# Second layer of a two-layer decoder trunk: where the value projection stands among the attention projections

## The chip, the cores and the metric

The kernel runs on one core of a Trainium2 chip. Its time is the device time of one execution in microseconds (us), and lower is better. Five engines work side by side, each through its own list of instructions in the order written: TensorE (PE; its weight loads are listed as PEld), VectorE (DVE), ScalarE (ACT), GpSimd (POOL) and SyncE (SP), which here issues transfers. What one engine needs from another it waits for.

## The reference, cut to what matters

Two layers with 512 tokens and width 1024, everything in float32. The change touches the second layer's mixer alone:

```python
proj = x @ od_w_in[o]
xr, gr, qd, kd, vd = split_cols(proj, [LRU_WIDTH, LRU_WIDTH, HALF, HALF, HALF])
yc = rg_lru_branch(xr, gr, ...)              # conv of width 4, two gates, linear scan, GeLU gate
yd = stick_breaking_attention(qd, kd, vd)    # 8 heads of 64
mix = jnp.concatenate([yc, yd], axis=-1) @ od_w_out[o]
...
# stick_breaking_attention, a block of 128 queries against the keys up to its end
z = einsum('bhqd,bhkd->bhqk', q, k) * scale
log_one_minus = where(mask, log_sigmoid(-z), 0.0)
suffix = cumsum(log_one_minus, reverse=True) - log_one_minus
w = where(mask, exp(log_sigmoid(z) + suffix), 0.0)
out = einsum('bhqk,bhkd->bqhd', w, v)
```

A head's sums z and their logarithms need only its q and k. The values v enter in the last product.

## The kernel before, in words

Every large product is made of three fp32r matmuls per 128-row block (`mm3`, L252 to L254): high by high, high by low, low by high. A weight chunk of 128 x 1024 arrives in `ws` (two buffers) by an SP transfer; ACT casts it to its high part (L241) and DVE subtracts to get the low part (L242). One projection of a chunk over all tokens (`proj`) is 24 matmuls of 128 x 512 into a PSUM bank `pj`, of which there are two. The value projection (`values`, L289 its copies) takes four chunks and is 96 such matmuls into banks `pv`, which share these two banks.

The second layer (`layer1`) runs as follows.

1. `griffin`, the recurrent branch. Four column groups j. Each has a convolution on DVE into a tile `xc` (L858, L860), two gate matmuls (`pa` L862, `px` L864), sigmoids and a tanh on ACT (L866 to L869), a logarithm part that goes back and forth between ACT (L882, L883, L889, L890) and DVE (L879, L884 to L894), a scan on DVE (L895), and, after one GeLU over all four groups on ACT (L900), a product, a cast and a subtraction (L907, L247, L248). PE makes the four `gr` projections meanwhile. `xc`, `dn` and `w` take their buffers from tag `l`, `r` from tag `z`.
2. The value projection.
3. Four pairs of heads (`sb_pair`). For each, `qk_pair` makes the q and the k projection and lays them out as `qk` tiles, with the low part of k in two `kz` tiles (L723 to L732: six instructions on ACT, four on DVE). The sums z of a pair are five tiles of 128 x 512. Each tile goes through z on PE (L933 to L935), three functions on ACT (L937 to L939), an addition, a reversed scan and a subtraction on DVE (L940, L943, L944), a "turn" (four PE transposes L951 into `pt`, an Exp on ACT L957 into `pT`), and then all five serve the products with v (L964).

The program is written in this order, and a scheduler then lists the instructions of each engine by its own estimate of when they can start; nothing reorders the list on the chip. The scheduler puts a pair's turns between the matmuls of the next pair's projections. A tile waits for its buffer until the last reader of the tile that had it is through.

Of the kernel before, what the change touches and what calls it, by code (L numbers as in the profile page):

```python
# [44 lines left out]
S_GR, S_QD, S_KD, S_VD, S_WO1 = S_XR + 4, S_XR + 8, S_XR + 12, S_XR + 16, S_XR + 20  # L45
# [11 lines left out]
class Trunk:  # L57
# [853 lines left out]
        return ys  # L911


    def sb_pair(self, hp, v):
        nc = self.nc
        A = nc.scalar.activation
        q, k = self.qk_pair(S_QD + hp, S_KD + hp, self.kz)
        yh, yl = self.act("yh"), self.act("yl")
        po = self.bank("ho", "po")


        tiles = (((0, 3, 0),), ((1, 3, 0),), ((0, 2, 0), (0, 0, 384)), ((1, 2, 0), (1, 0, 384)), ((0, 1, 0), (1, 1, 256)))
        pT = self.t2k("pT", [P, 20 * P], tag="pT")
        at = ((15, -6), (1, 5))
        rev = lambda a: a[:, ::-1]
        for ti, parts in enumerate(tiles):
            tag = "zl"[ti % 2]
            l = self.t2k("l", tag=tag)
            ps = self.bank(("s", "s", "sc")[ti % 3], "z")
            for e, i, o in parts:  # L930
                n = (i + 1) * P
                c = slice(i * P, n)
                nc.tensor.matmul(ps[:, o:o + n], q[e][:, c], k[e][:, 0:n], start=True, stop=False)  # L933
                nc.tensor.matmul(ps[:, o:o + n], q[e][:, c], self.kz[e][:, 0:n], start=False, stop=False)
                nc.tensor.matmul(ps[:, o + i * P:o + n], self.identb, self.sbmask, start=False, stop=True)  # L935

            A(l, ps, AF.Abs)  # L937
            A(l, l, AF.Exp, scale=-1.0)
            A(l, l, AF.Ln, bias=self.one)  # L939
            nc.vector.scalar_tensor_tensor(l, ps, 0.0, l, ALU.max, ALU.add)  # L940
            for e, i, o in parts:
                r = rev(l[:, o:o + (i + 1) * P])
                nc.vector.tensor_tensor_scan(r, self.ones1[:, 0:(i + 1) * P], r, 0.0, ALU.mult, ALU.add)  # L943
            nc.vector.tensor_tensor(l, ps, l, ALU.subtract)  # L944
            pt = self.bank(("pt", "po")[ti % 2], "pt")
            for e, i, o in parts:
                b, step = at[e]
                for j in range(i + 1):

                    m = j if step > 0 else i - j  # L950
                    nc.tensor.transpose(pt[:, o + m * P:o + (m + 1) * P], l[:, o + j * P:o + (j + 1) * P], self.ident)  # L951
            for e, i, o in parts:
                b, step = at[e]
                lo = b + i + (0 if step > 0 else i * step)
                dst = bass.AP(tensor=pT.tensor, offset=pT.offset + lo * P,
                              ap=[pT.ap[0], [abs(step) * P, i + 1], [1, P]])
                A(dst, pt[:, o:o + (i + 1) * P].rearrange("p (j t) -> p j t", t=P), AF.Exp)  # L957
        cp = self.newest()

        for j in range(NTB):  # L960
            for e in range(2):
                h = 2 * hp + e
                x = (at[e][0] + at[e][1] * j + j) * P
                nc.tensor.matmul(po[64 * e:64 * e + 64, j * P:T], v[j][:, h * 64:h * 64 + 64], pT[:, x:x + T - j * P],  # L964
                                 start=j == 0, stop=j == NTB - 1)
                if j == 0 and e == 0:
                    self.behind(self.newest(), cp)
        self.put(po, yh, yl)
        return yh, yl

    def layer1(self, xr):
        self.qk4 = False

        self.kz = [self.t2k("kz", dt=F32R, tag="kz") for _ in range(2)]
        for e in range(2):
            self.nc.gpsimd.memset(self.kz[e][64 - 64 * e:P - 64 * e].bitcast(F32), 0.0)
        self.ones1 = self.t2k("ones", tag="one")
        self.nc.gpsimd.memset(self.ones1, 1.0)
        yc = self.griffin(xr)
        self.hp = 600  # L980
        v = self.values(S_VD)
        self.hp = 600
        yd = []
        for hp in range(4):
            yd.append(self.sb_pair(hp, v))
            if hp == 3:
                self.out_rows(yc, S_WO1)
        self.hp = 1
        return yd


@with_exitstack
def hybrid_trunk_kernel(ctx: ExitStack, tc: tile.TileContext, out, **ins):
    t = Trunk(tc, ctx, ins, out)
    t.setup()
    with t.phase("l0", v=8, p=2, pT=1, E=5, bb=1, kq=1, G=1, acc=1, ks=1, es=1) as t.ph, \
            tc.tile_pool(name="odd", bufs=1) as t.odd:
        y = t.layer0()
    with t.phase("f0", s=2, d=1, fm=12, wah=4, wal=4) as t.ph:
        wa = t.out_rows(y, S_WO0 + 4, 0, S_FFN0)  # L1000
        wa = t.ffn(S_FFN0, wa, 1, S_XR)
        xr = t.proj_halves(wa)
    with t.phase("l1", v=4, qk=7, kz=2, z=5, l=4, pT=2, one=1) as t.ph:
        y = t.layer1(xr)
    with t.phase("f1", s=2, d=1, fm=12, wah=4, wal=4) as t.ph:
        wa = t.out_rows(y, S_WO1 + 4, 2, S_FFN1)
        t.ffn(S_FFN1, wa, 3)
# [105 lines left out]
```

## Time and profile before

| | |
|---|---|
| median of 3 runs | 1221.72 us (1219.8 to 1224.15) |
| the profiled execution | 1221.14 us, of which 1219.3 us lie between its first and last instruction |
| PE busy | 1196.5 us (98%) |
| DVE, ACT, POOL busy | 757.4 (62%), 518.6 (43%), 55.8 us (5%) |
| mean granted TensorE clock | 0.995 |
| second layer's mixer | griffin's gates from 676, value projection from 701, first pair's sums from 736 to 763, fourth pair's last products at 825 us |

How to read it: a line names the source line, the engine, the operation and what it writes and reads. Times in a timeline count from the span's start. Matmuls overlap in the record (one of 128 x 512 lasts 0.39 us, and the next starts 0.23 us after it), so the rate of work is read from starts. In the rows of stretches, the first number is the stretch's length, and behind it stands what each engine was busy in it, then the granted TensorE clock (1.00 is full), the share of the DMA engines and GB/s.

### The profile page before, as it was taken

Reading aid. Unit: us, or ns where it says so; the run is one execution under the profiler, and the core shown is the slowest. Engines: PE = TensorE matmul, PEld = TensorE weight load, DVE = VectorE, ACT = ScalarE, POOL = GpSimd, SP = SyncE. Lnnn points to the kernel's source line nnn. Section 1 sums busy time; section 2 is a strip of 40 time slices with the busy share of each in tenths; the row PEclk is TensorE's granted clock in tenths of the full one; section 3 lists DMA queues with packets and bytes.
Section 4 is the critical chain, followed back from the end, with each engine's and each line's share of the span. In section 5 each row is a group of like instructions: output and inputs, shape, how many; then the busy total and the mean of one; then the engine's idle time right before and its main releaser. Section 6 shows DMA issues by size and latency. Waiting matters only on the chain.

```text
span 1219.3 us, 15337 instructions
## 1 busy us (share of the span) xinstructions
PE 1196.5 (98%) x6063; PEld 970.6 (80%) x6063; DVE 757.4 (62%) x1141; ACT 518.6 (43%) x790; POOL 55.8 (5%) x80
## 2 busy tenths in 40 slices
PE   9999999999999999999999998999999999999997
PEld 6787777778888888878889786677988888888886
DVE  7638798769355634554368876887753644456346
ACT  7447568443233423332233667872332433333220
POOL 1000000001001000200000000000000100010001
PEclk9999999999999999999999999999999999999999
DMA  6421211233637432643324222112644643464321
GB/s 244 150 75 53 87 44 50 65 122 99 230 92 121 134 104 87 106 132 108 91 82 156 68 74 83 35 35 87 199 164 93 115 139 91 100 104 138 104 69 69
DMA packets 38727, 127.96 MB, mean 105 GB/s; under 512 B 4592, under 2 KB 6128, under 8 KB 38656
## 3 DMA queue, kind: packets, MB, share of 16 engines
q1 hardware_dynamic: 32496, 108.44, 28.0%
q0 software_dynamic: 4864, 16.81, 8.3%
q10 hardware_dynamic: 1296, 1.73, 0.4%
q8 instruction: 48, 0.79, 0.3%
q14 instruction: 23, 0.19, 0.1%
HBM read 124.84 MB, written 2.10 MB: 104 GB/s over the span
## 4 chain that ended last, share of the span: by engine, by line
PE 88%; DVE 4%; ACT 3%; DMA 2%; issue 1%; SPq 0%; DVEq 0%; ACTq 0%
PE pf L253 13%; PE pf L252 13%; PE pf L254 13%; PE pj L252 4%; PE pj L253 4%; PE pj L254 4%; PE po L254 4%; PE po L253 4%; PE po L252 4%; PE fa L252 2%; PE fa L254 2%; PE fa L253 2%; PE pv L253 2%; PE pv L252 2%; PE pv L254 2%; DMA wwal<-in_wst 1%
## 5 line engine op out<-in xcount | busy, mean ns | idle before, releaser
L241 ACT CAST wh<-ws 128x1024 fp32r<-128x1024 f32 x143 | 150.2, 1051 | 304.9 <-PE pf L253 121.8
L242 DVE TENSOR_TENSOR wl<-ws,wh 128x1024 fp32r<-128x1024 f32 x143 | 174.8, 1223 | 153.5 <-ACT wh L241 149.9
L252 PE MATMUL pf<-xh,wh 128*128 128x512 f32 x640 | 249.0, 389 | 0.0
L253 PE MATMUL pf<-xl,wh 128*128 128x512 f32 x640 | 249.0, 389 | 0.0
L254 PE MATMUL pf<-xh,wl 128*128 128x512 f32 x640 | 249.0, 389 | 0.0
L254 PEld LDWEIGHTS pf<-xh,wl 128*128 128x128 f32 x640 | 120.2, 188 | 25.0
L253 PEld LDWEIGHTS pf<-xl,wh 128*128 128x128 f32 x640 | 120.2, 188 | 24.9
L252 PEld LDWEIGHTS pf<-xh,wh 128*128 128x128 f32 x640 | 120.2, 188 | 24.7
L527 DVE TENSOR_TENSOR s<-s,pf 128x512 f32<-128x512 f32 x44 | 30.3, 688 | 148.0 <-PE pf L254 148.0
L252 PE MATMUL pj<-xh,wh 128*128 128x512 f32 x256 | 104.2, 407 | 2.1 <-DVE qk L726 2.1
L254 PE MATMUL pj<-xh,wl 128*128 128x512 f32 x256 | 104.0, 406 | 0.0
L253 PE MATMUL pj<-xl,wh 128*128 128x512 f32 x256 | 103.5, 404 | 0.2 <-DVE xl L248 0.2
L247 ACT CAST wh<-wwah 128x1024 fp32r<-128x1024 f32 x32 | 33.7, 1052 | 74.8 <-PE pf L253 63.3
L252 PEld LDWEIGHTS pj<-xh,wh 128*128 128x128 f32 x256 | 48.5, 190 | 13.6 <-DVE qk L726 2.6
L254 PEld LDWEIGHTS pj<-xh,wl 128*128 128x128 f32 x256 | 48.4, 189 | 10.3 <-issue 1.6
L253 PEld LDWEIGHTS pj<-xl,wh 128*128 128x128 f32 x256 | 48.5, 189 | 9.8 <-issue 1.0
L252 PE MATMUL po<-wh,yh 128*128 128x512 f32 x128 | 51.4, 401 | 0.0
L252 PE MATMUL fa<-wh,fm 128*128 128x512 f32 x128 | 50.0, 390 | 1.2 <-ACT wh L247 1.2
L253 PE MATMUL po<-wl,yh 128*128 128x512 f32 x128 | 51.0, 399 | 0.0
L254 PE MATMUL po<-wh,yl 128*128 128x512 f32 x128 | 50.9, 398 | 0.0
L248 DVE TENSOR_TENSOR wl<-wwah,wh 128x1024 fp32r<-128x1024 f32 x32 | 38.7, 1221 | 18.5 <-ACT wh L247 17.9
L254 PE MATMUL fa<-wh,fm 128*128 128x512 f32 x128 | 49.8, 389 | 0.0
(275 smaller groups left out, 2237.4 us busy)
## 6 DMA issues: line engine op xcount, KB each, us to landing
ws<-in_wst SPq DMA_DIRECT2D x165, 512.0 KB, 3.5
wwah<-in_wst POOLq DMA_DIRECT2D x24, 512.0 KB, 5.6
gb<-in_lnp SPq DMA_DIRECT2D x8, 512.0 KB, 5.1
wwah<-in_wst SPq DMA_DIRECT2D x8, 512.0 KB, 5.9
wwal<-in_wst SPq DMA_DIRECT2D x8, 512.0 KB, 6.8
wwal<-in_wst POOLq DMA_DIRECT2D x8, 512.0 KB, 6.1
ws<-in_wst SPq DMA_DIRECT2D x11, 256.0 KB, 5.2
xt<-in_xT SPq DMA_DIRECT2D x8, 256.0 KB, 5.2
```

The source lines that it names most:

```text
L241: nc.scalar.copy(hi, st)
L242: nc.vector.tensor_tensor(lo, st, hi.bitcast(F32), ALU.subtract)
L247: self.nc.scalar.copy(hi, dst)
L248: self.nc.vector.tensor_tensor(lo, dst, hi.bitcast(F32), ALU.subtract)
L252: mm(ps, ah, bh, start=first, stop=False, **kw)
L253: mm(ps, ah, bl, start=False, stop=False, **kw)
L254: mm(ps, al, bh, start=False, stop=last, **kw)
L527: nc.vector.tensor_tensor(h, h, pb, ALU.mult)
```

## The change

The first pair's projections and sums now stand ahead of the value projection, and so do the second pair's projections. `sb_pair` is called for pair 0 with a function `between`: the five z tiles are carried through their logarithms and kept; then `between` makes the second pair's `qk` tiles and the value projection; then the five turns follow. There are four `kz` tiles, two for even and two for odd pairs, and eight `qk` buffers instead of seven. Tag `z` has four buffers instead of five and tag `l` three instead of four, and the tile of ones that the scan read is gone: the scan reads a 128 x 1 column of ones, repeated.

```diff
-    def sb_pair(self, hp, v):
+    def sb_front(self, hp):
+        return self.qk_pair(S_QD + hp, S_KD + hp, self.kz[hp % 2])
+
+    def sb_pair(self, hp, v, front=None, between=None):
...
-        q, k = self.qk_pair(S_QD + hp, S_KD + hp, self.kz)
+        q, k = front or self.sb_front(hp)
+        kz = self.kz[hp % 2]
...
+        def turn(ti, parts, l):
+            pt = self.bank(("pt", "po")[ti % 2], "pt")
...
-                nc.vector.tensor_tensor_scan(r, self.ones1[:, 0:(i + 1) * P], r, 0.0, ALU.mult, ALU.add)
+                nc.vector.tensor_tensor_scan(r, self.one.to_broadcast([P, (i + 1) * P]), r, 0.0, ALU.mult, ALU.add)
...
+            if between:
+                ls.append((ti, parts, l))
+            else:
+                turn(ti, parts, l)
+        if between:
+            v = between()
+            for x in ls:
+                turn(*x)
...
-        self.kz = [self.t2k("kz", dt=F32R, tag="kz") for _ in range(2)]
...
+        self.kz = [[self.t2k("kz", dt=F32R, tag="kz") for _ in range(2)] for _ in range(2)]
...
         yc = self.griffin(xr)
         self.hp = 600
-        v = self.values(S_VD)
...
+        def between():
+
+            front.append(self.sb_front(1))
+            v.extend(self.values(S_VD))
+            return v
+
         for hp in range(4):
-            yd.append(self.sb_pair(hp, v))
+            yd.append(self.sb_pair(hp, v, front[0] if hp == 1 else None, between if hp == 0 else None))
...
-    with t.phase("l1", v=4, qk=7, kz=2, z=5, l=4, pT=2, one=1) as t.ph:
+    with t.phase("l1", v=4, qk=8, kz=4, z=4, l=3, pT=2) as t.ph:
```

How the lists of the engines stand. The first place is PE, from griffin's last projection (`pj_944`) to the first sums of pair 0 (`z_990`), before; `pv_969` and `pv_972` are the first and the last bank of the value projection, `pj_980` and `pj_984` the first pair's projections of q and k, `pj_1011` the second pair's q.

```order
L254 MATMUL pj_944_5773<-xh_83,wl_943_5770 128x512
L252 MATMUL pv_969_5849<-wh_958_5827,xh_83 128x512
...
L254 MATMUL pv_972_5927<-wh_967_5845,xl_84 128x512
L252 MATMUL pj_980_5963<-xh_83,wh_978_5959 128x512
...
L254 MATMUL pj_984_5998<-xh_83,wl_983_5995 128x512
L252 MATMUL pj_1011_6153<-xh_83,wh_1009_6149 128x512
...
L933 MATMUL z_990_6034<-qk_975_5955,qk_973_5953 128x512
```

In this list the value projection and two chunks' projections, 144 matmuls, lie between griffin's last projection and the second pair's q, and nine more ahead of the first sums. The same place of the changed kernel: `pj_945` is griffin's last projection, `pj_961` and `pj_965` the first pair's q and k, `z_971` its first sums, `pj_987` the second pair's q.

```order
L254 MATMUL pj_945_5775<-xh_83,wl_944_5772 128x512
L252 MATMUL pj_961_5833<-xh_83,wh_959_5829 128x512
...
L254 MATMUL pj_965_5868<-xh_83,wl_964_5865 128x512
L954 MATMUL z_971_5904<-qk_956_5825,qk_954_5823 128x512
L954 MATMUL z_975_5926<-qk_956_5825,qk_954_5823 128x384
L252 MATMUL pj_987_5980<-xh_83,wh_985_5976 128x512
L253 MATMUL pj_987_5980<-xl_84,wh_985_5976 128x512
L254 MATMUL pj_987_5980<-xh_83,wl_986_5977 128x512
L955 MATMUL z_971_5904<-kz_888_5503,qk_954_5823 128x512
```

Now 48 matmuls lie between griffin's last projection and the first sums, and the second pair's q stands behind these.

The second place is PE around the value projection (`pv_1008` to `pv_1011`) of the changed kernel. `pt_1012` to `pt_1016` are the five turns of pair 0, `z_1022` the first sums of pair 1.

```order
L254 MATMUL pj_991_6015<-xh_83,wl_990_6012 128x512
L938 MATMUL pt_1012_6178<-ident_66,l_970_5903 128x128 x4
L938 MATMUL pt_1013_6184<-ident_66,l_972_5914 128x128 x4
L938 MATMUL pt_1014_6190<-ident_66,l_974_5925 128x128 x4
L938 MATMUL pt_1015_6197<-ident_66,l_976_5940 128x128 x4
L954 MATMUL z_1022_6226<-qk_982_5972,qk_980_5970 128x512
L954 MATMUL z_1028_6260<-qk_982_5972,qk_980_5970 128x384
L938 MATMUL pt_1016_6204<-ident_66,l_978_5955 128x128
L252 MATMUL pv_1008_6074<-wh_997_6052,xh_83 128x512
...
L254 MATMUL pv_1011_6152<-wh_1006_6070,xl_84 128x512
L938 MATMUL pt_1016_6204<-ident_66,l_978_5955 128x128 x3
L955 MATMUL z_1022_6226<-kz_890_5505,qk_980_5970 128x512
```

Four of the five turns, and the start of the fifth, stand ahead of the 96 matmuls of the value projection; the completion of pair 1's first sums stands behind them.

The third place is DVE at griffin's end. Before, its last instructions were followed by the splitting of weights:

```order
L895 SCALAR_TENSOR_TENSOR ig_899_5544<-w_928_5658,ig_899_5544 128x512
L248 TENSOR_TENSOR yl_946_5803<-ig_899_5544,yh_945_5802 128x512
L907 TENSOR_TENSOR ig_899_5544<-ig_899_5544,ig_900_5545 128x512
...
L248 TENSOR_TENSOR yl_952_5818<-ig_899_5544,yh_951_5817 128x512
L242 TENSOR_TENSOR wl_983_5995<-ws_981_5992,wh_982_5994 128x1024
```

Nothing but griffin's own work stood there. Now the list holds a third value chunk's split (`wl_1004`) and the second half of q (`qk_955`) between them, and the low parts of k (`kz_888`, `kz_889`) directly behind:

```order
L895 SCALAR_TENSOR_TENSOR ig_900_5546<-w_929_5660,ig_900_5546 128x512
L242 TENSOR_TENSOR wl_1004_6065<-ws_1002_6062,wh_1003_6064 128x1024
...
L248 TENSOR_TENSOR yl_951_5815<-ig_900_5546,yh_950_5814 128x512
L726 SCALAR_TENSOR_TENSOR qk_955_5824<-pj_961_5833,qk_955_5824 64x512
L248 TENSOR_TENSOR yl_953_5820<-ig_900_5546,yh_952_5819 128x512
L732 TENSOR_TENSOR kz_888_5503<-pj_965_5868,qk_956_5825 64x512
L732 TENSOR_TENSOR kz_889_5504<-pj_965_5868,qk_957_5826 64x512
```

From griffin's first L884 to the last `yl`, DVE splits two weight chunks before the change and four after it, and two L726 are new in that stretch.

More of the change, by code (lines that the diff above doesn't have):

```diff
@@ L925, in sb_pair @@
         rev = lambda a: a[:, ::-1]
[L926 to L944, printed above, removed]
+        def turn(ti, parts, l):
             pt = self.bank(("pt", "po")[ti % 2], "pt")
@@ L957, in sb_pair @@
                 A(dst, pt[:, o:o + (i + 1) * P].rearrange("p (j t) -> p j t", t=P), AF.Exp)
+        ls = []
+        for ti, parts in enumerate(tiles):
+            tag = "zl"[ti % 2]
+            l = self.t2k("l", tag=tag)
+            ps = self.bank(("s", "s", "sc")[ti % 3], "z")
+            for e, i, o in parts:
+                n = (i + 1) * P
+                c = slice(i * P, n)
+                nc.tensor.matmul(ps[:, o:o + n], q[e][:, c], k[e][:, 0:n], start=True, stop=False)
+                nc.tensor.matmul(ps[:, o:o + n], q[e][:, c], kz[e][:, 0:n], start=False, stop=False)
+                nc.tensor.matmul(ps[:, o + i * P:o + n], self.identb, self.sbmask, start=False, stop=True)
+            A(l, ps, AF.Abs)
+            A(l, l, AF.Exp, scale=-1.0)
+            A(l, l, AF.Ln, bias=self.one)
+            nc.vector.scalar_tensor_tensor(l, ps, 0.0, l, ALU.max, ALU.add)
+            for e, i, o in parts:
+                r = rev(l[:, o:o + (i + 1) * P])
+                nc.vector.tensor_tensor_scan(r, self.one.to_broadcast([P, (i + 1) * P]), r, 0.0, ALU.mult, ALU.add)
+            nc.vector.tensor_tensor(l, ps, l, ALU.subtract)
+            if between:
[6 more added lines that the diff above has]
+                turn(*x)
         cp = self.newest()
@@ L972, in layer1 @@
         self.qk4 = False
-        self.kz = [self.t2k("kz", dt=F32R, tag="kz") for _ in range(2)]
[L975 to L978, printed above, removed]
+        self.kz = [[self.t2k("kz", dt=F32R, tag="kz") for _ in range(2)] for _ in range(2)]
+        for kz in self.kz:
+            for e in range(2):
+                self.nc.gpsimd.memset(kz[e][64 - 64 * e:P - 64 * e].bitcast(F32), 0.0)
         yc = self.griffin(xr)
         self.hp = 600
-        v = self.values(S_VD)
-        self.hp = 600
-        yd = []
+        yd, v, front = [], [], []
+        def between():
+            front.append(self.sb_front(1))
+            v.extend(self.values(S_VD))
+            return v
         for hp in range(4):
-            yd.append(self.sb_pair(hp, v))
+            yd.append(self.sb_pair(hp, v, front[0] if hp == 1 else None, between if hp == 0 else None))
             if hp == 3:
```

## The prediction

> **What bounds the kernel now.** First the page's head and the list of waits on PE.
>
> ```profile
> span 1219.3 us, 15337 instructions
> PE 1196.5 (98%) x6063; PEld 970.6 (80%) x6063; DVE 757.4 (62%) x1141; ACT 518.6 (43%) x790; POOL 55.8 (5%) x80
> PE pt L951 <- DVE l L944: 4.6, 9, 0.8
> PE pj L252 <- DVE qk L726: 2.1, 1, 2.1
> ```
>
> PE is busy throughout; 22.8 us of the span are idle on it. The two longest waits are the second layer's: turns that wait for DVE's logarithms, and one projection that waits until its PSUM bank is read by L726. Matmuls cannot get fewer by this change, so all that it can move is PE's idle time. I therefore read the second layer stretch by stretch.
>
> ```profile
> 690.00:701.05 11.05, 11.05 (x51) 9.14 (x49) 9.53 (x15) 6.63 (x12) 0.00 (x0) 1.00 0.26 90
> 701.05:711.95 10.90, 10.90 (x49) 8.74 (x47) 10.87 (x20) 10.70 (x14) 0.00 (x0) 1.00 0.17 53
> 711.95:723.11 11.16, 11.16 (x50) 9.12 (x49) 8.67 (x12) 5.77 (x9) 0.00 (x0) 1.00 0.06 7
> 736.31:763.12 26.81, 22.66 (x114) 15.94 (x114) 19.82 (x29) 20.07 (x36) 0.00 (x0) 0.94 0.19 60
> 763.12:782.48 19.36, 18.13 (x100) 13.05 (x98) 16.11 (x23) 15.36 (x28) 0.00 (x0) 1.00 0.13 32
> 782.48:805.38 22.90, 21.27 (x115) 15.21 (x113) 18.92 (x26) 18.43 (x34) 0.00 (x0) 1.00 0.20 64
> 752.00:756.00 4.00, 0.93 (x5) 0.61 (x5) 3.64 (x6) 3.78 (x7) 0.00 (x0) 1.00 0.19 33
> 757.40:760.80 3.40, 3.40 (x13) 2.29 (x12) 1.55 (x3) 2.55 (x6) 0.00 (x0) 0.52 0.00 0
> ```
>
> Pair 0 (736.31 to 763.12) loses 26.81 - 22.66 = 4.15 us on PE, pairs 1 and 2 lose 1.23 and 1.63. Pair 0 also loses clock: after the sparse 752 to 756, 3.4 us run at 0.52, which is 3.4 x 0.48 = 1.6 us of work. So at most 5.75 us can be won there. The value projection (701.05 to 723.11) has no idle time, and it is not empty cover: in its first half DVE is busy 10.87 of 10.90 us and ACT 10.70. It hides the end of griffin.
>
> **The change: the first sums lose this cover.** What feeds them now:
>
> ```profile
> 701.05 0.39 PE L252 MATMUL pv<-wh,xh 128*128 128x512 f32 x1
> 723.11 0.39 PE L252 MATMUL pj<-xh,wh 128*128 128x512 f32 x1
> 692.66 0.68 DVE L884 TENSOR_TENSOR dn<-dn,w 128x512 f32<-128x512 f32 x1
> 716.80 1.47 DVE L248 TENSOR_TENSOR yl<-ig,yh 128x512 fp32r<-128x512 f32 x2
> 710.15 1.28 ACT L903 ACT_TABLE_LOAD   x1
> 736.35 0.68 DVE L732 TENSOR_TENSOR kz<-pj,qk 64x512 fp32r<-64x512 f32 x1
> 696.95 1.22 DVE L242 TENSOR_TENSOR wl<-ws,wh 128x1024 fp32r<-128x1024 f32 x1
> 698.08 0.42 DVE L894 TENSOR_SCALAR w<-w 128x512 f32<-128x512 f32 x1
> 729.63 0.68 DVE L726 SCALAR_TENSOR_TENSOR qk<-pj,qk 64x512 fp32r<-64x512 f32 x1
> ```
>
> *PE's arrival.* 96 matmuls take 723.11 - 701.05 = 22.06 us, 0.23 each. In place of `pv` the first pair's 48 projection matmuls start at 701.05 and are through at 701.05 + 48 x 0.23 = 712.1; with 0.5 us from the smaller tag (below), 712.6. The next instructions in PE's list are the sums z of pair 0.
>
> *When their operands are there.* ACT makes the k tiles only behind griffin's GeLU, table load and first casts, of which the table load ends at 710.15 + 1.28 = 711.4 today. DVE makes `kz` directly behind griffin's last `yl`, which ends at 716.80 + 1.47 = 718.27. From the first L884 at 692.66 to there DVE has 25.6 us, almost all busy, so what is added there is paid: two more L242 (one starts at 696.95 and the instruction behind it at 698.08, so 1.13 us each) and two L726 (0.68 long, 0.60 with the same overlap), which is 3.46 us, so 29.1.
>
> *The start moves too.* With three `l` buffers griffin's fourth `xc` must wait for the first to be read.
>
> ```profile
> 673.22 4.03 DVE L860 SCALAR_TENSOR_TENSOR xc<-xp,par,xc 128x511 f32<-128x511 f32 x6
> 682.53 0.68 DVE L871 TENSOR_TENSOR ig<-ig,xc 128x512 f32<-128x512 f32 x1
> 684.39 0.42 DVE L879 TENSOR_SCALAR dn<-r 128x512 f32<-128x512 f32 x1
> 687.41 0.67 ACT L868 ACTIVATE ig<-px,par 128x512 f32<-128x512 f32 x1
> 691.39 0.63 ACT L883 ACTIVATE w<-w 128x512 f32<-128x512 f32 x1
> ```
>
> DVE reads the first `xc` at 682.53. From there to the end of the fourth `xc` the new list has this read, two more like it, three L860 (4.03 / 6 = 0.67 each) and three short ones like L879; at 0.6, 0.67 and 0.35 apiece that is 4.9 us, so about 687.4. Its gate matmuls (about 0.9 us) and three ACT functions of 0.6 to 0.7 then end at about 690.1 instead of 687.41 + 0.67 = 688.1. The following L883 thus falls 2.0 us later than 691.39, and the first L884 with it: 694.7. PE loses little of this, since ten matmuls are listed ahead of the late gates: 0.5 us is my estimate, between 0 and the whole 2.0.
>
> So `kz` is ready at 694.7 + 29.1 + 0.7 = 724.5. Until then PE has two first parts of z and three matmuls of the second pair's q, five of 0.23, so 1.2 us. **New wait at the first sums: 724.5 - 712.6 - 1.2 = 10.7 us.** Behind the waiting z stand the second pair's 48 matmuls and the 96 of `pv`, which need nothing that is late; the list is fixed, so they wait, and with them ACT's copies of v and all later products. Bounds: with no extra DVE work and no late start, `kz` is there at 719.0 and PE at 712.1, so 719.0 - 712.1 - 1.2 = 5.7; with 2 us of bubbles where a DVE instruction needs the one just ahead of it, 12.7.
>
> *Pair 0's own chain.* It now runs under the second pair's 48 projection matmuls, as it did before, and not under the value projection: four of five turns stand ahead of `pv`. Only the last turn's exponentials and the products are covered. So PE waits there again, less than 4.15 us, since the last turn is no longer waited for, and hardly less than pair 1's 1.23. I take 3.0, nearer to pair 0's row, because the next work and the chain are the same; both ends stay in the range. During `pv` itself ACT and DVE will be nearly idle.
>
> *The clock.* The row at 752 shows what about 4 us of thin work is followed by: 3.4 us at half clock. A wait of 10.7 us should bring that at least once: 1.6 us, nothing if that stretch waits for DVE anyway, 3.3 if it comes twice.
>
> [...]
>
> *Edits that I cost at nothing.* The scan's ones: a scan reads 512 elements in 1.22 us, a product of two tiles in 0.68.
>
> ```profile
> 741.86 1.23 DVE L943 TENSOR_TENSOR_SCAN l<-ones,l 128x512 f32<-128x512 f32 x1
> L907 DVE TENSOR_TENSOR ig<-ig,ig 128x512 f32<-128x512 f32 x4 | 2.7, 680 | 0.0
> ```
>
> It is slower than its reads, so a repeated column should not change it; were it as much as 10% slower or faster, 20 full-length scans' worth of work (2560 elements per pair, 24.6 us in all) would move by 2.5 us on DVE, part of it in front of turns, which the range holds. Two more `kz` memsets for one of the ones lie on POOL, which is busy 55.8 us in all. Transfers keep their number and places in SP's list; only the chunks in them change order. Four `z` and eight `qk` buffers: a pair holds three `z` and four `qk`, and the list of the later pairs is nearly the old one, so nothing.
>
> Sum: 10.7 + 0.5 + 3.0 + 1.6 - 5.75 = **+10.05 us**. On the profiled execution's own 1221.14 us that is 1231.2; it stands 0.6 below the median of 1221.72, so I say 1231.
>
> **The rivals.**
>
> *Faster: the value projection covers the chain.* If `kz` were ready when PE arrives, nothing would be waited for at the first sums, and pair 0 would lose what pair 1 loses: 1.23 - 5.75 = -4.5, 1216.6. For it: pair 0's chain is the layer's worst stretch, and 22 us without a wait are moved. Against it: DVE would have to be through 12 us earlier, with 10.87 of 10.90 us filled. It decides where the wait at the first sums falls below 4.5 us; even the lower bound is 5.7.
>
> *No change.* The wait at its lower bound 5.7, pair 0 like pair 1 and no half clock: 5.7 + 1.23 - 5.75 = +1.2, 1222.3. For it: the scheduler's list interleaves, so DVE could find room; against it: the two splits and two L726 are listed ahead of `kz`.
>
> *Much worse: griffin starves on three `l` tiles, and the clock stays low.* `dn` and `w` of two groups need four. If each later group waits once more for its buffers, `kz` comes 2 us later still; with 2.0 on PE from the fourth `xc`, 4.15 kept and half clock twice: 12.7 + 2.0 + 4.15 + 3.3 - 5.75 = +16.4, 1237.5. For it: ACT already waits 4.08 us for DVE there with four tiles.
>
> ```profile
> 701.20 0.64 ACT L882 ACTIVATE w<-dn 128x512 f32<-128x512 f32 x1 [4.08 <-DVE dn L879]
> ```
>
> Against it: DVE is the busy engine, and reordering its work does not lengthen it. [...]
>
> *That the change doesn't do what it says* holds in part: the second pair's sums are not ahead, only their first parts, as the list shows. This is in the 3.0 above.
>
> **How the numbers follow.** Forecast 0.70; much worse 0.15; no change 0.08; faster 0.07. Both of the first are slower: 0.85. A change under 0.3% (3.7 us) cannot be told from none: 1218.1 to 1225.4. The range that should hold the time 8 times in 10 runs from 1224.5, which takes in part of the case of no change, to 1237, just under the worst case; the forecast's own range is 1227 to 1235.
>
> **What would show it.** In the changed kernel's profile: a PE wait of 8 to 12 us at the first z (L954 or L955), ended by ACT's k tile (L731) or DVE's `kz` (L732), near 713 to 724; the last `yl` of griffin at 722 to 724 instead of 718.3; a stretch of granted clock near 0.5 just behind it and none near 757; DVE and ACT nearly idle for 15 us under `pv`; pairs 1 to 3 as now. I am wrong if PE's wait at the first sums is under 5 us, if the turns ahead of `pv` cost more than 4 us, or if the scan's duration changes.

## The result and the profile after

The changed kernel takes 1230.83 us (median of 6 runs, 1230.22 to 1232.97); the kernel before, run beside it, 1221.11 us (median of 6, 1218.68 to 1224.15). The ratio is 1.0083 with a 95% interval of 1.0066 to 1.0099: slower, by 9.7 us, where +10.05 had been forecast.

The profiled execution took 1232.97 us. First its page's head and the longest waits of PE in the second layer (us in total, times, longest).

```profile
span 1231.2 us, 15345 instructions
PE 1199.1 (97%) x6063; PEld 972.7 (79%) x6063; DVE 757.9 (62%) x1141; ACT 518.0 (42%) x790; POOL 55.3 (4%) x81
PE z L954 <- ACT qk L731: 10.4, 2, 8.9
PE pt L938 <- DVE l L965: 4.2, 10, 0.8
```

The work is the same, and a wait that no row of before has heads the list. Its 10.4 us lie in two places: 8.92 us at the first sums, and the rest, 1.45 us, at pair 1's first sums (at 746.43). At the first sums a second wait follows, of 1.05 us. Here is PE at that place, and the copy on ACT that it first waits for:

```profile
722.73 1.11 PE L954 MATMUL z<-qk,qk 128*128 128x512 f32 x2 [8.92 <-ACT qk L731]
724.89 0.77 PE L252 MATMUL pj<-xh,wh 128*128 128x512 f32 x1 [1.05 <-DVE qk L726]
726.31 0.77 PE L955 MATMUL z<-kz,qk 128*128 128x512 f32 x1
722.10 0.58 ACT L731 CAST qk<-pj 64x512 fp32r<-64x512 f32 x1
```

So PE stands still for 8.92 + 1.05 = 9.97 us: first for ACT's copy of k, then for the PSUM bank that DVE's L726 has still to read. Ahead of the first matmul with `kz` (L955) there is no wait. The expectations of e2, e5, e6 and e8 call this wait 10.4 us; that is the sum over both places. To see what it is worth, the same work is cut out of both: from the start of griffin's first product into `px` (677.63 us before, 678.87 after) to the first product with v of pair 1. The stretches of before, from the start of `pv` on, and the whole:

```profile
701.05:736.31 35.26, 35.14 (x154) 28.38 (x153) 25.81 (x37) 23.61 (x31) 0.00 (x0) 1.00 0.28 91
736.31:760.81 24.50, 20.35 (x97) 14.87 (x97) 18.71 (x27) 18.97 (x35) 0.00 (x0) 0.93 0.21 65
760.81:780.13 19.32, 18.09 (x98) 12.80 (x97) 15.98 (x23) 14.87 (x28) 0.00 (x0) 1.00 0.10 28
677.63:780.13 102.50, 97.00 (x438) 72.89 (x436) 79.79 (x117) 75.02 (x120) 0.00 (x0) 0.98 0.21 67
```

And of after, cut where PE arrives at the first z (713.81), where its first matmul with `kz` starts (726.31), where `pv` starts (747.20) and where pair 0's products start (770.33):

```profile
678.87:702.29 23.42, 23.32 (x89) 16.40 (x88) 17.94 (x28) 17.46 (x27) 0.00 (x0) 1.00 0.18 53
...
713.81:726.31 12.50, 2.53 (x5) 1.36 (x6) 12.05 (x19) 9.34 (x12) 0.00 (x0) 0.69 0.18 59
726.31:747.20 20.89, 18.12 (x88) 13.50 (x87) 16.48 (x24) 15.94 (x28) 0.00 (x0) 0.94 0.10 27
747.20:770.33 23.13, 23.13 (x105) 18.80 (x105) 3.80 (x4) 6.50 (x13) 0.00 (x0) 1.00 0.13 44
770.33:791.84 21.51, 19.89 (x108) 15.02 (x107) 18.92 (x25) 17.51 (x32) 0.00 (x0) 1.00 0.32 100
678.87:791.84 112.97, 98.50 (x440) 74.28 (x438) 80.71 (x117) 74.71 (x120) 0.00 (x0) 0.95 0.20 61
```

The same work takes 112.97 - 102.50 = 10.47 us more. Of this PE is idle for 14.47 instead of 5.50 us, 8.97 more, and busy for 1.50 us more, of which the half clock is 0.85 (worked out below, with the prediction). Behind this stretch nothing more is lost: from there to the last matmul it is 431.3 us before and 431.5 after. Under the value projection (747.20 to 770.33) PE is full, and DVE with 3.80 of 23.13 us and ACT with 6.50 have next to nothing to do. The 22 us that hid griffin's end now hide little.

The profiled execution is 2 us above the median of its kernel; 1.24 us of that (678.87 - 677.63) are there by griffin's first gate, ahead of all that the change touches. Of this 1.0 us is there after 20 us, where PE in this execution waited 0.8 and 0.3 us for its first casts; across the first layer's half clock, 6.83 us in this execution (from 237.37) and 3.41 in the one of before (from 238.41), 1.1 more is added, and 0.9 goes off again by 677.

### The profile page after: what moved, and what is told of

Same layout as the page of the kernel before. It is cut to its first block, busy times and chain, and to the rows that moved or that the text cites. A ratio compares the mean times of both kernels' runs of the same rounds, so it can differ in the third digit from the quotient of the medians.

```text
span 1231.2 us, 15345 instructions
## 1 busy us (share of the span) xinstructions
PE 1199.1 (97%) x6063; PEld 972.7 (79%) x6063; DVE 757.9 (62%) x1141; ACT 518.0 (42%) x790; POOL 55.3 (4%) x81
## 4 chain that ended last, share of the span: by engine, by line
PE 87%; DVE 7%; ACT 3%; DMA 2%; issue 1%; SPq 0%; DVEq 0%; ACTq 0%
PE pf L253 13%; PE pf L252 13%; PE pf L254 13%; PE po L254 4%; PE po L253 4%; PE po L252 4%; PE pj L252 4%; PE pj L253 4%; PE pj L254 4%; PE fa L252 2%; PE fa L254 2%; PE fa L253 2%; PE pv L253 2%; PE pv L252 2%; PE pv L254 2%; DVE l L964 1%
## 5 line engine op out<-in xcount | busy, mean ns | idle before, releaser
L254 PEld LDWEIGHTS pj<-xh,wl 128*128 128x128 f32 x256 | 48.4, 189 | 10.6 <-issue 1.8
```

What stands on the lines that cost most here:

```text
L254: mm(ps, al, bh, start=False, stop=last, **kw)
```

## The experiments

The theory: the value projection covered the end of griffin on DVE and ACT; with the sums ahead of it, PE waits about 10 us at the first z. Two rivals stand against it: the buffers (three `l`, the scan over one repeated column), and the turns, which are held back behind five sums. Another question is asked by itself: how much of the loss is the half clock. Line numbers in the experiments' rows can lie a few lines off those above, since each kernel has its own text.

All medians, beside those of the kernel before on the same chip, with the profiled stretch from the start of the first `px` to the start of the last matmul (before: 533.8 us), which leaves out what differs ahead of griffin's gates:

| kernel | us | before | ratio, 95% interval | `px` to the end, against before |
|---|---|---|---|---|
| the change | 1230.83 | 1221.11 | 1.0083 (1.0066 to 1.0099) | +10.6 |
| e1, tiles alone | 1220.06 | 1220.40 | 1.0000 (0.9990 to 1.0009) | 0.0 |
| e3, values first | 1219.44 | 1220.40 | 0.9997 (0.9987 to 1.0006) | +0.2 |
| e2, four logs | 1227.81 | 1220.40 | 1.0058 (1.0043 to 1.0073) | +7.9 |
| e6, late splits | 1230.31 | 1220.65 | 1.0075 (1.0062 to 1.0089) | +10.2 |
| e8, drains first | 1224.87 | 1220.15 | 1.0044 (1.0031 to 1.0056) | +5.4 |
| e5, wait filled | 1231.04 | 1220.15 | 1.0094 (1.0079 to 1.0109) | +10.3 |
| e4, values split | 1232.49 | 1220.40 | 1.0098 (1.0083 to 1.0113) | +12.1 |
| e9, split, other banks | 1223.09 | 1220.15 | 1.0024 (1.0015 to 1.0032) | +1.8 |
| e10, and drains first | 1220.42 | 1220.15 | 0.9999 (0.9990 to 1.0008) | -0.1 |
| e11, and second front | 1219.19 | 1220.65 | 0.9987 (0.9978 to 0.9996) | -1.9 |
| e12, second front last | 1218.10 | 1220.65 | 0.9978 (0.9969 to 0.9987) | -2.1 |
| e13, late fourth sum | 1217.16 | 1220.47 | 0.9972 (0.9962 to 0.9981) | -2.9 |

### Is it the order? The tiles alone, and the values put back

```diff
 # e1: the changed kernel, in the old order
-            yd.append(self.sb_pair(hp, v, front[0] if hp == 1 else None, between if hp == 0 else None))
+        v = self.values(S_VD)
+            yd.append(self.sb_pair(hp, v))
 # e3: the changed kernel, with the values ahead of everything
-        yd, v, front = [], [], []
+        yd, v, front = [], self.values(S_VD), []
-            v.extend(self.values(S_VD))
```

> The changed kernel's tiles (two sets of key tiles, eight q and k buffers, four of the sums' z, three of the logs, and the running sum that multiplies by the one repeated column), in the old order: griffin, the value projection, then pair after pair. Theory (the value projection used to hide griffin's tail, and the order alone lost it): 1221 to 1224 us, that is 0 to 3 us over the kernel before, with no wait over 2 us at the first z and the one half-rate stretch about where it was, near 757 us. Rival (the smaller set of log buffers and the repeated column make the kernel slower, by late griffin gates and longer scans): 1228 us or more, and the running sum of 512 columns takes longer than its 1.23 us.

> The change with one thing put back: the value projection comes ahead of the first pair's projections and sums again. What stays of the change is its tiles, the five sums in a row, the second pair's projections behind them and the five turns last. Theory: the value projection covers griffin's tail as before, the wait at the first z is under 2 us, and pair 0's own waits for logs are shorter: 1219 to 1224 us. Rival (holding the turns back behind five sums, or the second pair's early projections, cost the time): 1226 us or more, with the loss between pair 0's sums and its outputs.

Both came out as the theory says: no difference from the kernel before. PE in the 34 us from 711 to 745 of e1, and of e3:

```profile
711.00:745.00 34.00, 33.58 (x154) 26.82 (x154) 23.07 (x29) 24.17 (x36) 0.00 (x0) 1.00 0.33 108
```

```profile
711.00:745.00 34.00, 33.48 (x152) 26.73 (x151) 23.08 (x29) 23.89 (x35) 0.00 (x0) 1.00 0.33 106
```

PE is busy for all but half a microsecond, where the changed kernel loses 11.31 us of the same window:

```profile
711.00:745.00 34.00, 22.69 (x101) 16.47 (x99) 29.21 (x44) 25.12 (x37) 0.00 (x0) 0.85 0.16 47
```

So the tiles cost nothing under the old cover, and neither do the turns held back. e1 also has the repeated column: its scan of 512 elements takes 1.22 us (1.23 with the tile of ones).

```profile
739.23 1.22 DVE L964 TENSOR_TENSOR_SCAN l<-one,l 128x512 f32<-128x512 f32 x1
```

e3 gains nothing either, although pair 0's four waits before its turns are gone. PE's list of waits of e3 between 660 and 800 us is headed by one at another place, the first z of pair 1:

```profile
PE z L954 <- ACT qk L731: 3.3, 1, 3.3
```

### How much is the late start, how much the two splits?

```diff
 # e2: the changed kernel
-    with t.phase("l1", v=4, qk=8, kz=4, z=4, l=3, pT=2) as t.ph:
+    with t.phase("l1", v=4, qk=7, kz=4, z=4, l=4, pT=2) as t.ph:
 # e6: the changed kernel
+            self.hp = 1
             v.extend(self.values(S_VD))
+            self.hp = 600
```

In e6, `hp` is the priority that the casts and splits of weights get when the lists are made.

> The change with a fourth log buffer, paid for with the eighth q and k buffer. Griffin's last gates have their buffer as in the kernel before and should come early again, and later turns are no longer held by a log buffer. Theory (the loss is the uncovered wait at the first z): still slower than before, about 1226 to 1229 us: the wait at the first z is about 2 us shorter (some 8 us where it was 10.4), and the turns' own waits of 2 to 3 us go. Rival (the three log buffers are the cause): 1222 us or less, with a wait at the first z under 3 us.

> The changed kernel with the priority of the value weights' splits taken away: on VectorE the second of the two splits that came into the stretch before kz now stands behind it, and the first a little later. Theory (each split of 1.13 us that stands ahead of kz lengthens the wait by as much): the wait at the first z is 9.0 to 9.6 us where it was 10.4, and the time 1229 to 1230.5 us. Rival (splits of value weights that come late hold up the value projection, which then waits for its weights): a new wait of PE at the first value block, and 1231.5 us or more.

e2 took 1227.81 us, 7.4 above before, as expected; the wait, expected at 8 us, is 9.85. The list differs: the second pair's q projection now stands ahead of the first sums, and the wait sits there, since its PSUM bank is still to be read by L726, which stands behind griffin's last `yl` on DVE. PE, and then DVE, of e2:

```profile
720.75 0.76 PE L252 MATMUL pj<-xh,wh 128*128 128x512 f32 x1 [9.85 <-DVE qk L726]
719.19 0.69 DVE L248 TENSOR_TENSOR yl<-ig,yh 128x512 fp32r<-128x512 f32 x1
719.91 0.69 DVE L726 SCALAR_TENSOR_TENSOR qk<-pj,qk 64x512 fp32r<-64x512 f32 x1
```

Griffin's last `yl` starts at 719.19, 42.9 us behind the `px` of this run (676.34), where the changed kernel has 724.78 - 678.87 = 45.9. The fourth buffer is worth 3 us on DVE, and 2.3 (medians against before) to 2.7 us (the table's last column) in the time, with the eighth `qk` buffer given up for it and the list changed along with it. The rival, which put the whole loss on the three buffers, falls; that they are 2 to 3 of the 10 us, where no cover stands above them, remains.

In e6 the first `kz` came 721.76 - 676.60 = 45.2 us behind `px` in place of 725.48 - 678.87 = 46.6, 1.4 us earlier:

```profile
718.39 1.11 PE L954 MATMUL z<-qk,qk 128*128 128x512 f32 x2 [6.88 <-ACT qk L731]
721.15 0.77 PE L252 MATMUL pj<-xh,wh 128*128 128x512 f32 x1 [1.65 <-DVE qk L726]
```

The two waits at the first sums are 6.88 + 1.65 = 8.53 us in place of 9.97, also 1.4 less. The split that moved behind `kz` is worth 1.13 us of this; what gave the other 0.3 is not shown. The time was within the expectation and hardly better, 1230.31 us. The gain was lost again in the value projection: its 96 matmuls take 21.66 us from the first start to the last in the changed kernel (747.20 to 768.86), and 23.26 here. In e6's stretch from the first `pv` the granted clock is not full:

```profile
743.54:767.00 23.46, 23.46 (x96) 19.21 (x97) 4.40 (x5) 5.48 (x9) 0.00 (x0) 0.93 0.08 25
```

A stretch of 3.4 us at half clock had fallen onto full work there, 0.07 x 23.46 = 1.6 us. So in e6 the place of the half clock took back what the shorter wait had brought, 1.6 us against 1.4.

### Is it that the lists of DVE and ACT have the drains behind griffin's tail?

The first sums need no product of griffin. They need the copies that drain the first pair's projections from PSUM, and these stand behind griffin's last products and splits in the lists of DVE and ACT. e8 gives these ten copies priority when the lists are made:

```diff
+        with self.tc.high_priority(offset=ahead):
             for e, d in enumerate(hv):
                 nc.scalar.mul(qs[e][d], qp[d], 0.125)
...
-        return self.qk_pair(S_QD + hp, S_KD + hp, self.kz[hp % 2])
+        return self.qk_pair(S_QD + hp, S_KD + hp, self.kz[hp % 2], ahead=1 if hp else 600)
```

> The changed kernel with the copies that drain the first pair's q and k projections given priority, so that on VectorE the two low halves of q and the two of k come ahead of griffin's last products and splits instead of behind them; the last gates also come early again. Nothing else is added or left out. Theory (the first z waits for the low half of k only because that stands behind griffin's tail in VectorE's order): kz is ready near 714 us, the wait at the first z is 2 to 4 us where it was 10.4, and the time 1220 to 1223 us. Rival (VectorE simply has too much to do before the first sums, so the wait moves to the next z or to its logs): 1226 us or more.

1224.87 us lies between the two expectations, and the trace has both halves. PE of e8:

```profile
717.48 0.47 PE L957 MATMUL z<-kz,qk 128*128 128x512 f32 x1 [1.19 <-DVE kz L734]
732.48 0.66 PE L956 MATMUL z<-qk,qk 128*128 128x384 f32 x1 [4.79 <-DVE l L967]
736.23 0.55 PE L956 MATMUL z<-qk,qk 128*128 128x256 f32 x1 [1.22 <-DVE l L967]
```

The waits at the first sums fell from 9.97 us to 1.45 (1.19, and 0.26 at the second pair's q, not printed) by giving ten instructions in two lists priority, so that it was one of order is shown. Which of the two lists alone would have done it is not, since both moved. But z has three PSUM banks, and the fourth sum waits until the first has been read by its logarithm's last step (L967 here), which is still behind griffin's tail:

```profile
727.35 0.69 DVE L248 TENSOR_TENSOR yl<-ig,yh 128x512 fp32r<-128x512 f32 x1 [0.34 <-ACT yh L247]
728.07 0.69 DVE L963 SCALAR_TENSOR_TENSOR l<-z,l 128x512 f32<-128x512 f32 x1
731.05 0.68 DVE L248 TENSOR_TENSOR yl<-ig,yh 128x512 fp32r<-128x512 f32 x1
731.65 0.68 DVE L967 TENSOR_TENSOR l<-z,l 128x512 f32<-128x512 f32 x1
```

So DVE is through in time for the first three sums, and not for all five. 5 of 10 us come back.

### What does the half clock cost?

e5 adds 34 matmuls that nothing reads behind the first pair's k projection, so that PE is not idle while it waits.

```diff
+            for _ in range(fill):
+                nc.tensor.matmul(dump, self.xh[:, 0, 0:P], self.xh[:, 0, :], start=True, stop=True)
+                self.behind(self.newest(), last)
```

> The changed kernel with 34 extra matmuls whose result nothing reads, behind the first pair's k projection: they keep TensorE busy for about 8 of the 10.4 us that it waits at the first z. The wait itself stays, since it is for VectorE. Theory (the half-rate stretch of 10.24 us behind the wait costs about 1.5 to 2.5 us): no half-rate stretch near 720 to 730 us, and 1228.3 to 1229.5 us. Rival (the clock costs nothing there, because the first sums wait for VectorE anyway): 1230.5 us or more.

1231.04 us: no gain, as the rival has it, but the question stays open, because the half clock did not go. Three stretches of e5, the last one from the first `pv` on:

```profile
720.00:723.40 3.40, 1.64 (x6) 1.16 (x7) 3.23 (x6) 1.40 (x3) 0.00 (x0) 1.00 0.18 75
723.40:726.80 3.40, 3.40 (x12) 2.25 (x11) 1.00 (x2) 1.82 (x4) 0.00 (x0) 0.50 0.00 0
744.38:767.60 23.22, 23.22 (x97) 19.09 (x97) 4.40 (x5) 5.77 (x10) 0.00 (x0) 0.94 0.07 21
```

The first sums themselves fill only 1.64 of 3.40 us, and 3.4 us at 0.50 followed. A second such stretch fell into the value projection (0.94 over 23.22 us). The value projection started 68.0 us behind `px` (744.38 - 676.43), 0.3 earlier than in the changed kernel (747.20 - 678.87), and took 1.4 us longer from its first start to its last (23.02 and 21.66). The changed kernel by stretches of 3.41 us:

```profile
718.65:722.06 3.41, 0.00 (x0) 0.00 (x0) 3.41 (x6) 2.62 (x5) 0.00 (x0) 0.50 0.20 34
722.06:725.48 3.42, 1.70 (x4) 1.03 (x5) 3.25 (x5) 1.79 (x4) 0.00 (x0) 0.50 0.30 120
725.48:728.89 3.41, 3.41 (x12) 2.31 (x11) 1.38 (x2) 2.28 (x5) 0.00 (x0) 0.50 0.00 0
728.89:732.30 3.41, 3.41 (x16) 2.60 (x16) 1.05 (x2) 2.92 (x7) 0.00 (x0) 1.00 0.00 0
```

Three of them ran at half clock (0.50). The first was idle, the second half full (1.70 of 3.42 us), and only behind the third, the first full one (3.41 of 3.41), the clock rose to 1.00.

### Can the sums come early and keep a cover?

Three kernels split the value projection: first pair's projections, value blocks 0 and 1 of four, the five sums, blocks 2 and 3, the turns. They have the tiles of the kernel before. A dependence (`behind`, not printed) keeps the sums behind block 1 in PE's list.

```diff
 # e4
+        front = self.qk_pair(S_QD, S_KD, self.kz)
+        self.tok_blocks(vw, (0, 1), sink)
+        def between():
+            self.tok_blocks(vw, (2, 3), sink)
 # e9: as e4, and
-            ps = self.bank("g", "pv")
+            ps = self.bank(("pt", "po")[tb] if free and tb < 2 else "g", "pv")
 # e10: as e9, and the drains of e8
+        front = self.qk_pair(S_QD, S_KD, self.kz, ahead=600)
```

> The kernel before with its own tiles and another order: the first pair's q and k projections, two of the four token blocks of the value projection, the five sums, the other two value blocks, then the turns. Theory (about 11 us of value projection are enough to cover griffin's tail, and the other 11 cover the running sums and logs that pair 0 waits for): wait at the first z at most 2 us, pair 0's waits mostly gone and no half-rate stretch near 757 us: 1216 to 1220 us. Rival (splitting the projection gains nothing since waits only move): 1221 us or more.

> The split value projection once more, with its first two blocks in the two PSUM banks of the turns, which are free then, in place of the two banks that the first pair's projections still hold. Theory (in the earlier split the first value block waited 9.9 us for a bank whose reader stands behind griffin's tail on VectorE, so nothing covered the tail): no wait at the first value block, 1 to 2 us at the first z, and 1216 to 1219 us. Rival (the split itself, or the sums so close behind griffin, cost the time): 1226 us or more.

> The split value projection in the free banks, and the first pair's drains ahead of griffin's tail on VectorE. Theory: no wait over 1 us at the first value block or the first z, pair 0's waits for logs mostly gone: 1215 to 1218 us, up to 2 us below the split alone. Rival (the first two value blocks already cover what the drains gain): the same as the split in other banks within 1 us.

e4 was a clear miss, 1232.49 us. It is the wait of e2 once more: the first value block needs a bank that the drain has not read.

```profile
721.28 0.76 PE L252 MATMUL pv<-wh,xh 128*128 128x512 f32 x1 [9.88 <-DVE qk L729]
```

Work that is meant as a cover must not need what it is to cover. In e9 the two blocks have banks of their own and the wait is gone (PE's waits at the first z are 0.6 and 0.3 us), with 9 us won back. Yet neither e9 nor e10 is faster than the kernel before, where 1 to 5 us had been expected. The reason is in PE's later rows; first of e10, then of before, with its waits ahead of pair 0's turns:

```profile
762.44 0.66 PE L938 MATMUL pt<-ident,l 128*128 128x128 f32 x4 [0.28 <-DVE l L967]
767.33 0.66 PE L938 MATMUL pt<-ident,l 128*128 128x128 f32 x4 [0.70 <-DVE l L967]
771.55 0.63 PE L938 MATMUL pt<-ident,l 128*128 128x128 f32 x4 [1.01 <-ACT wh L241]
774.27 0.51 PE L252 MATMUL pj<-xh,wh 128*128 128x512 f32 x1 [2.09 <-DVE qk L730]
```

```profile
743.87 0.66 PE L951 MATMUL pt<-ident,l 128*128 128x128 f32 x4 [0.35 <-DVE l L944]
748.76 0.66 PE L951 MATMUL pt<-ident,l 128*128 128x128 f32 x4 [0.69 <-DVE l L944]
752.98 0.63 PE L951 MATMUL pt<-ident,l 128*128 128x128 f32 x4 [1.02 <-ACT wh L241]
755.70 0.50 PE L252 MATMUL pj<-xh,wh 128*128 128x512 f32 x1 [2.09 <-DVE qk L726]
```

The four waits are the same to a few hundredths, 4.15 us in sum before and 4.08 in e10, but at pair 1's turns instead of pair 0's. They are the price of the first pair whose successor's projections start only with its turns, and the split gave pair 1 that role. That is the 4 us that had been counted as a gain. Why e9 is 2.9 us above before, and not level as e10, is seen only in part: its two short waits at the first z, and 6.8 us of half clock at pair 1's turns (0.83 over the 20 us from 770) where e10 had 3.4 (from near 775.1 to 778.5).

The change has the remedy for this in itself: the second pair's projections come early. e11 and e12 join it to e10, with the changed kernel's tiles; e13 moves the last two sums.

```diff
 # e11                                          # e12: the two lines in the other order
+        def between():
+            front.append(self.sb_front(1))
+            self.tok_blocks(vw, (2, 3), sink)
 # e13: as e12, the fourth and fifth sum behind value block 3
+            if after and ti == 3:
+                after = middle()
```

> The changed kernel's tiles and its early second projections, but with the first pair's drains ahead of griffin's tail, the first two value blocks (in the two free banks) ahead of the sums and the other two behind the second pair's projections. Theory (the uncovered tail was the change's only cost; the waits of 4.1 us in pair 0's turns, which the split alone only moved to pair 1, are what the early second projections take away): no wait over 1 us at the first z, pair 0's and pair 1's waits under 2 us together, 1214.5 to 1217.5 us. Rival (those waits move on to pair 2 or 3, or three log buffers bring as much back): 1219 us or more.

> As the kernel with the split and the early second projections, but with the second pair's projections behind the last two value blocks in place of ahead of them. Theory (either stretch of 11 us covers pair 0's logs, and the projections that come last leave pair 1's drains less cover before its sums): 1215 to 1219 us, 0 to 1.5 us above the other order. Rival (waits only move): 1219 us or more in both.

> The kernel with the split and the second pair's projections behind the last two value blocks, with one thing moved: the fourth and the fifth sum come behind the last value block in place of in the midst of the third, so that the PSUM bank that the fourth needs is free by then. Theory (the 2.35 us wait of the fourth z for the first log, and the one half-rate stretch behind it, are what is left of griffin's tail): no wait over 0.5 us at the fourth z and no half-rate stretch near 736 us: 1214 to 1216.5 us. Rival (the logs of the last two sums then come too late for the turns, and the wait turns up there): 1217.5 us or more, with new waits over 1 us at pair 0's turns.

All three are faster than the kernel before, by 0.13, 0.22 and 0.28%, and their intervals stay below 1. e11 is above what the theory expected and just inside its rival: its first z does not wait, but its fourth does, for 2.35 us. e12 has the same wait; it is where the theory put it, but 1.1 us below e11 and not above, with intervals that overlap. What e12 had left of griffin's tail, and what e13 made of it, each with the row of the 34 us:

```profile
731.72 0.41 PE L959 MATMUL z<-qk,qk 128*128 128x384 f32 x1 [2.35 <-DVE l L972]
711.00:745.00 34.00, 31.66 (x142) 25.50 (x141) 29.30 (x41) 25.22 (x37) 0.00 (x0) 0.95 0.17 53
```

```profile
711.00:745.00 34.00, 34.00 (x160) 27.75 (x159) 26.97 (x39) 26.56 (x38) 0.00 (x0) 1.00 0.22 72
749.40 0.47 PE L252 MATMUL pj<-xh,wh 128*128 128x512 f32 x1 [2.63 <-DVE qk L730]
```

e13 fills the stretch to the last hundredth, with DVE 26.97 of 34 us busy beside it. A wait of 2.63 us turned up in the second pair's projections instead, with 3.4 us of half clock behind it, which is the rival's kind of outcome at another place than it named. So of e12's 2.35 us little is kept: the median of 1217.16 us lies between the two expectations, and e12 and e13 cannot be told apart by their intervals. By its ratio e13 is 0.28% below the kernel before, where the change is 0.83% above it.

## Why the prediction was right, step by step

The measured stretches go against the terms of its sum, all in us of PE; the profiled times of after are lowered by the 1.24 us that are there by griffin's first gate.

| step of the prediction | said | measured |
|---|---|---|
| PE arrives at the first sums | 712.6 | 713.81 - 1.24 = 712.6 |
| start of the first L884, with three `l` buffers | 694.7 | 695.66 - 1.24 = 694.4 |
| from there to griffin's last `yl` on DVE | 29.1 | 725.47 - 695.66 = 29.8 |
| first `kz` there | 724.5 | 726.16 - 1.24 = 724.9 |
| new wait at the first sums | 10.7 | 12.50 - 2.53 = 10.0 |
| late gates | 0.5 | 0.1 |
| pair 0's chain | 3.0, was 4.15 | 2.77, of other waits |
| pair 1 | 1.23 as before | 1.62 |
| clock | 1.6, was 1.6 | 2.55, was 1.70, in what PE is busy |
| more waits, whose edges count as busy | nothing | about 0.64 |
| sum | +10.05 | +10.47 |

The rows for the second to fourth line of it, DVE of the changed kernel:

```profile
695.66 0.69 DVE L884 TENSOR_TENSOR dn<-dn,w 128x512 f32<-128x512 f32 x1 [0.96 <-ACT w L883]
724.78 0.69 DVE L248 TENSOR_TENSOR yl<-ig,yh 128x512 fp32r<-128x512 f32 x1
725.48 0.68 DVE L732 TENSOR_TENSOR kz<-pj,qk 64x512 fp32r<-64x512 f32 x1
```

*The cover.* Right in mechanism and in size, but not in its last link. e1 and e3 show that the order is the cause, e8 that the place of ten copies in two lists is. The prediction let PE do the first parts of z and three q matmuls while it waited, and put the end of the wait at `kz`. In the trace the first part of z itself waits until 722.73, for ACT's copy L731. The prediction had named the work ahead of this copy, but took the table load in it at today's 711.4; it ended at 717.60 + 1.28 = 718.88, 6.2 us later when lowered by the 1.24. Then q waits until 724.89 for L726 on DVE. `kz` is ready at 726.16, within 0.4 us of the forecast, but PE is at the q matmuls until 726.31, at half clock; with 0.23 us apiece it would have been through at 724.89 + 0.69 = 725.6 and waited for `kz`. That the sum over DVE alone gave the length, though ACT was late by nearly as much, is in part luck. The last `yl` ended at 725.47 - 1.24 = 724.2, which is 0.2 us outside the stretch named for it, because the DVE work took 0.7 us longer than the added instructions. PE was idle 0.7 us less than said, because 2.53 us of z and q matmuls ran in the stretch, at half clock, where 1.2 had been counted at full.

*Late gates.* Mis-sized by 0.4 us: matmuls listed ahead of them hid the delay on PE, which was busy for 23.32 of the 23.42 us from 678.87 to 702.29. On DVE the three `l` buffers were worth 3 us at the last `yl` (e2), a little more than the 2.0 of the prediction.

*Pair 0's chain.* The size, 2.77, is nearly right, and by luck. It had been argued that the chain would run under the second pair's projections as before and so keep most of its waits. None of before's four waits is left in that stretch: the 2.77 us are 1.45 at pair 1's first z, which waits for ACT's copy of k, 0.37 and 0.42 at two of pair 0's own sums, and 0.53 at a turn. That the old 4.15 us are what the first pair without early successor projections pays, wherever that pair stands (e9, e10), was not seen.

*The clock.* Half clock came for 10.24 us where one stretch had been counted, but it cost less than that length suggests. Its stretches hold 1.70 + 3.41 = 5.11 us in which PE worked, half of which, 2.55, is put down to the granted 0.50 as the clock's share of PE's busy time; before it was half of 3.41, so 1.70. The matmuls bear this out nearly: those at 725.46, 725.88 and 726.31 start 0.42 and 0.43 us apart, where it is 0.23 at full clock. The other 0.65 of the 1.50 us more is not the clock's. After has ten waits of PE over 0.2 us from `px` to pair 1's products, before six, and the last matmul ahead of a wait shows its whole 0.39 us, where the next one follows after 0.23 otherwise: four times 0.16 is 0.64 us. The prediction put this at nothing. And 2.53 us of the half clock's work lie ahead of 726.31, where DVE had `kz` ready only at 726.16 whatever PE's clock. Only the 2.56 us from there to the clock's rise at 728.87 can have cost time, at most 1.3 us by this working, where the prediction said 1.6. Its own condition, that the stretch costs nothing while it waits for DVE, came true for half of it. What a kernel without it would gain no run shows, since e5 did not get rid of it.

*At nothing.* The scan with the repeated column (1.23 us at 731.94, as before), the `kz` tiles, the `z` and `qk` buffers: e1 bears it out, 1.0000 with 0.9990 to 1.0009.

*The rivals.* Faster needed the first `kz` when PE arrives, no change a wait of half the size; the matmul with `kz` started 12.50 us behind PE's arrival. Of the much worse case the longer half clock came true, though not its price, and the starving griffin did not: DVE was busy for 12.05 of the 12.50 us of the wait, with the longer list and not with gaps.

*The sum* is 0.42 us low. Its terms are off by -0.7 (wait), -0.4 (gates), -0.2 (pair 0) and +0.4 us (pair 1), and by +0.85 (clock) and +0.64 us (edges of waits), which in part cancel; 0.12 us of idle time that before had up to its first sums goes off as well. That the total came so near is therefore in part luck.

## What to carry to other kernels

A long product that keeps TensorE full may be the cover under which other engines finish the stage before; look at what DVE and ACT do under it before you move it, and at what stands ahead of the next stage's first copies in their lists. A cover counts only if it needs none of the buffers that the late engine has still to free (e4's waited 9.88 us for one). A wait that disappears in one place should be looked for at the next iteration, with its old length (4.15 us before, 4.08 in e10), before it is booked as a gain.

## What the runs showed that was not expected

A stretch of TensorE need not be idle to be followed by half clock: behind 1.64 us busy of 3.40 (720.00 to 723.40) it came in e5, and in e12 behind a single gap of 2.35 us. What decides it these runs do not show. In e6, 1.91 us busy of 3.41 (740.27 to 743.68) were followed by half clock, in the changed kernel 1.92 (742.53 to 745.94) were followed by 1.00. In e2 1.52 (709.38 to 712.79) were not followed by it at once either: 0.85 over its 34 us from 711 to 745 is 10.2 us of half clock, and its matmuls are at full rate again from near 726.4, so that by this working it began near 716.2. So the busy share of one stretch does not decide it alone. Half clock came in stretches of 3.41 us (before, from 238.41 and from 757.24), 6.83 (the changed kernel, from 237.37) and 10.24 (there, over the wait), apart from that at the kernel's end. The clock rose again behind 3.41 us busy of 3.41 in the changed kernel (725.48 to 728.89), behind 3.40 of 3.40 in e5 (723.40 to 726.80). In these runs where it fell mattered more than how long it was: of the 10.24 us over the wait of the change at most 1.3 us can have been lost by the working above, and 3.4 us that fell into the full value projection cost 1.6 (e6).
